# A hybrid decoder step: the bonus product placed behind the transposes, longer step distances, and a memory operand that takes over the input operand's halves

## Chip, cores and metric

The kernel runs on one core of one Trainium2 chip. The metric is the device time of one execution in microseconds (us); of several runs the median is given.

## The reference, cut to what matters here

One decoder layer for 256 prompt tokens and 8 sequences of 8 new tokens (320 tokens, 2048 wide). One projection with `w_in` gives the columns of a convolution group and of a time-mix group; their outputs are joined, projected, and followed by cross-attention into 256 memory tokens and a gated FFN. The change touches the time-mix group, whose 16 heads of 64 columns run a recurrence, and the memory keys:

```
def wkv_step(S, inp):
    r, w, k, v, a, b = inp
    sa = jnp.einsum('bhij,bhj->bhi', S, a)
    S = S * w[:, :, None, :] + sa[..., None] * b[:, :, None, :] + v[..., None] * k[:, :, None, :]
    y = jnp.einsum('bhij,bhj->bhi', S, r)
    return S, y
...
bonus = jnp.sum(rh * kh * heads(jnp.broadcast_to(p['r_k'].astype(f32), r.shape)), axis=-1, keepdims=True) * vh
out = (yn + bonus.reshape(b_, t_, W)) * g
...
def memory_kv(mem, p):
    m = rms_norm(mem, p['norm_mem'])
    k = (m @ p['w_k']).reshape(b_, N_MEM, XA_HEADS, XA_HEAD_DIM)
    v = (m @ p['w_v']).reshape(b_, N_MEM, XA_HEADS, XA_HEAD_DIM)
```

## The kernel before

**Weights.** Every large product is float32 carried as two float16 parts. A piece of a weight, 128 x 1024 float32, is loaded by SP into one of three buffers of the tag `raw`; ACT rounds it to `whi` (L154) and DVE computes the remainder `wlo` (L155). PE then runs three matmuls per 128 x 128 block: high by high, high by low, low by high (`dense_steps`, result `acc`). The input operand `h1`, transposed and split the same way, holds 16 blocks of 320 tokens in one tile.

**The recurrence** (L364 to L1073, about 95 to 705 us of the span) is one block in which the order of PE is the order in which the program issues instructions; the other engines and SP's queue are ordered by the framework's scheduler. Two things are interleaved there. The main line is dense work: `weights` (L1040) runs, four times, the r, k and v columns of two head pairs (`columns`) and two convolution blocks of 128 columns (`conv_dense`); then `memory` (L1046) runs the memory tokens' transposes (`memo_steps`, L903, PE result `pm`, split by ACT L918 and DVE L919 into `memo`) and the products with `w_k` (`mem_steps`, L928, result `acck`). The small work runs as streams: generators that issue a few instructions and then `yield d`, the step distance. A counter `clock[0]` advances with every matmul by its modelled length, and a stream is resumed between two dense steps once the counter has passed its last stop plus d. So a distance is PE work put between a product and the next product that needs what other engines make of it. When the real engines take longer than the distance, PE waits, since its order is fixed.

**The streams.** `prepare` (L482) makes the operands of one pair of heads, eight times: among them `kt` (POOL, L561), the bonus operand `k` (DVE, L562), `kh` (DVE, L570 and L571), then the bonus product

```
        yield 9.12
        pb_ = etile("pbon")
        mm(pb_[:, :T], bones, k2, True, True)
        bon = rb.tile([P, T], F32, tag="bon", bufs=3, name="bon")
        V.tensor_tensor(bon, pb_[:, :T], v, ALU.mult)
```

and then the transposes `px` of v and kt, of bt, and of v's and kh's sample columns. `etile` hands out one single PSUM bank (tag "x", one buffer), which every product of `prepare` uses in turn: the next one can start when the last has been read. `mtile` hands out five banks (tag "m"). `pair` (L595) runs the recurrence of a pair in chunks of 64 tokens: `invert` (L364; `psZ`, then DVE `zc`, then `psX`, then DVE `Tc` L400 and its transposition L401, four levels for the prompt), `prompt_part` (L661; four chunks of `pX`, ACT `x`, `pU`, DVE `u` L679, `pSc`), `sample_part` (L708) and the output (`pYt`). Two pairs are under way at a time, each of the two streams doing four pairs. The convolution's taps (DVE, L821, 31 for each of 8 blocks) are streams as well.

**The turn to the memory products.** When `conv_dense(7)` has been issued, a tile `memo` takes the place of `h1` in memory, so its first write has to wait until the last product has read `h1`. `memory` then issues four steps of transposes, each followed by `clock[0] += 1.0`, then the `w_k` products with the four other steps between them. The memory tiles `xm` use the same three `raw` buffers as the weights; the rest of the tile (`kvst`) holds results on the way out.

Of the kernel before, what the change touches and what calls it, by code (L numbers as in the profile page):

```python
# [9 lines left out]
F32 = mybir.dt.float32  # L10
# [36 lines left out]
def hybrid_step_kernel(ctx: ExitStack, tc: tile.TileContext, I, O):  # L47
# [137 lines left out]

    def opn(t):
        return lambda k: (t[:, k, 0, :], t[:, k, 1, :])

# [5 lines left out]
    def rows_in(pool, psum, loads, gcol, op, ssq, take):  # L194
        tl = []
        for j, (src, rows) in enumerate(loads):
            tl.append((pool.tile([P, D], F32, name=f"xt{j}"), rows))
        for q in range(4):
            qc = slice(q * 512, (q + 1) * 512)
            with tc.high_priority(offset=(2 * AHEAD if q == 0 else AHEAD)):  # L200
                for (xt, rows), (src, _) in zip(tl, loads):
                    SP.dma_start(xt[:rows, qc], src[:, qc])
            with tc.high_priority(offset=600):
                for f in range(4 * q, 4 * q + 4):
                    ps = psum.tile([P, 512], F32, tag="m", bufs=5, name="psn")
                    c = 0
                    for xt, rows in tl:
                        turn(ps[:, c:c + rows], xt[:rows, f * P:(f + 1) * P], ident[:rows, :rows])
                        c += rows
                    A.activation(op[:, f, 0, :c], ps[:, :c], AF.Copy, scale=gcol[:, f:f + 1])  # L210
                    V.scalar_tensor_tensor(op[:, f, 1, :c], ps[:, :c], gcol[:, f:f + 1], op[:, f, 0, :c], ALU.mult, ALU.subtract)
            take(q)
            for j, (xt, rows) in enumerate(tl):
                jk = pool.tile([P, 512], F16, tag="njk", bufs=2, name="njk")
                sq = A.activation(jk[:rows], xt[:rows, qc], AF.Square, accum_out=ssq[:rows, j, q:q + 1])
                if q in (0, 1, 2, 3):
                    late(sq)
# [4 lines left out]
    opA = tc.alloc_tile_pool(name="opA", bufs=1, side="right")  # L222
    h1 = opM.tile([P, KD, 2, T], F16, tag="h", name="h1")
    rwmix = opA.tile([P, 8, 2, T], F16, name="rwmix")
# [6 lines left out]
    with tc.tile_pool(name="p0", bufs=1, side="right", reuse_waits="tile") as p0:  # L231
# [12 lines left out]
        xp, xs_ = I["x_prompt"][0], I["x_sample"].rearrange("b t d -> (b t) d")  # L244
        rows_in(p0, psA, [(xp[0:128], 128), (xp[128:256], 128), (xs_, 64)], gx[:, 0:16], h1, xss, lambda q: [next(first_) for _ in range((8, 8, 8, 0)[q])])
        ldm = vr.tile([26, P], F32, name="ldm")
# [117 lines left out]
    def invert(A_, GG, nm, C, nlev):  # L364
# [17 lines left out]
        for lev in range(1, min(nlev, 5)):  # L382
# [10 lines left out]
            V.tensor_tensor(zm, psZ[:C, :nm * 16].rearrange("p (a c) -> p a c", c=16), CM[:C, lev].unsqueeze(1).broadcast_to([C, nm, 16]), ALU.mult)  # L393
            yield 3.16
            psX = mtile("psX")
# [5 lines left out]
            V.transpose(Gf, Tf)  # L401
            yield 3.78
        for q, r in enumerate(blk):
# [78 lines left out]
    def prepare(i, r, k, v):  # L482
# [79 lines left out]
        V.scalar_tensor_tensor(k2, r, vR["r_k"][:, c], k2, ALU.mult, ALU.mult)  # L562
        yield 9.12
        pb_ = etile("pbon")
        mm(pb_[:, :T], bones, k2, True, True)
        bon = rb.tile([P, T], F32, tag="bon", bufs=3, name="bon")
        V.tensor_tensor(bon, pb_[:, :T], v, ALU.mult)
        pcs = PS[:, :, 8:9].broadcast_to([P, NB, NT])
        kh = ra.tile([P, 2, NS], F32, tag="kh", name="kh")
        V.tensor_tensor(kh[:, 0].rearrange("p (b e) -> p b e", e=NT), sm(kt), pcs, ALU.mult)  # L570
        V.tensor_tensor(kh[:, 1].rearrange("p (b e) -> p b e", e=NT), sm(bt), pcs, ALU.mult)  # L571
        yield 0.71

# [5 lines left out]
        A.activation(tvkb[:, 0:2].rearrange("p z c f -> p (z c f)"), px, AF.Copy)  # L579
        yield 1.39  # L580
        px = etile("px")
        for ch in range(2):
            turn(px[:, ch * P:(ch + 1) * P], bt[:, ch * P:(ch + 1) * P], ident)
        A.activation(tvkb[:, 2].rearrange("p c f -> p (c f)"), px[:, 0:256], AF.Copy)
        yield 1.21

# [4 lines left out]
        A.activation(ts_[0:64, 0], px[0:64, 0:P], AF.Copy)  # L591
        A.activation(ts_[:, 1], px[:, P:2 * P], AF.Copy)
        return AR, bt, kt, bon, tvkb, ts_, pc

    def pair(i, AR, bt, kt, bon, tvkb, ts_, pc):  # L595
# [65 lines left out]
        def prompt_part():  # L661
            Sbd = Ssc = None
            for ch in range(4):
# [9 lines left out]
                A.activation(x[xr_], px[xr_, 0:P], AF.Copy)  # L673
                yield 1.5
                pu = mtile("pU")
# [5 lines left out]
                for hc in hcs:  # L681
                    mm(ps[hc, 0:64], tk[xr_, m, hc], tv[xr_, m, hc], True, False, True, 2)
                yield 1.1
                for hc in hcs:
# [13 lines left out]
                A.activation(Y[yr_, m, :], px[yr_, 0:P], AF.Copy)  # L698
                yield 1.5
            px = mtile("pSt")  # L700
# [200 lines left out]

    mst = cst.tile([P, 2, 8], F32, name="mst")
    def memo_steps():  # L903
        for q2 in range(2):
            for j in range(2):
                with tc.high_priority(offset=AHEAD):
# [4 lines left out]
                for q in range(2 * q2, 2 * q2 + 2):  # L911
                    px = mtile("pm")
                    for z in range(4):
                        turn(px[:, z * P:(z + 1) * P], xm[:, (4 * (q % 2) + z) * P:(4 * (q % 2) + z + 1) * P], ident)
                    cols = slice(j * P, (j + 1) * P)
                    for z in range(4):
                        f = 4 * q + z
                        A.activation(memo[:, f, 0, cols], px[:, z * P:(z + 1) * P], AF.Copy, scale=gx[:, 16 + f:17 + f])  # L918
                        V.scalar_tensor_tensor(memo[:, f, 1, cols], px[:, z * P:(z + 1) * P], gx[:, 16 + f:17 + f],  # L919
                                               memo[:, f, 0, cols], ALU.mult, ALU.subtract)  # L920
                    yield
# [6 lines left out]
    def mem_steps(src, dst, ns, psum):  # L928
        for n in ns:
            accs = [psum.tile([P, 512], F32, tag="acc", name="acck", **({"bufs": 2} if psum is psA else {})) for _ in range(2)]  # L930
            for k0 in range(0, KD, 2):
                hi, lo = wpiece(src, k0, 2, [(n * 512, 512)])
                for j in range(2):
                    for k in range(2):
                        kt, c, cols = k0 + k, slice(k * 512, (k + 1) * 512), slice(j * P, (j + 1) * P)
                        mm(accs[j], memo[:, kt, 0, cols], hi[:, c], kt == 0, False)
                        mm(accs[j], memo[:, kt, 1, cols], hi[:, c], False, False)
                        mm(accs[j], memo[:, kt, 0, cols], lo[:, c], False, kt == KD - 1)
                        yield 1.5
            for j in range(2):  # L940
                kv = kvst[:, j]
                A.activation(kv, accs[j], AF.Copy, scale=mst[:, j, 7:8])  # L942
# [97 lines left out]
    def weights():  # L1040
        for q in range(4):
            yield from columns(q)
            yield from conv_dense(2 * q)
            yield from conv_dense(2 * q + 1)

    def memory():  # L1046
        ms, ks = memo_steps(), mem_steps(I["w_k"][0], O[10], range(4), psA)
        for _ in range(4):
            next(ms)
            clock[0] += 1.0  # L1050
            yield
        for n in range(32):
# [12 lines left out]
    with tc.manual_schedule(engines={mybir.EngineType.PE}):  # L1065
        for a_ in (first_stage(), second_stage(0), second_stage(1)):
            spawn(a_)
        drive(weights())
        hm_ = opM.tile([P, KD * 2 * T], F16, tag="h", name="memo")
        memo = hm_[:, 0:KD * 2 * NPR].rearrange("p (k y t) -> p k y t", y=2, t=NPR)  # L1070
        kvst = hm_[:, KD * 2 * NPR:].bitcast(F32).rearrange("p (j c) -> p j c", c=512)
        drive(memory())
# [568 lines left out]
```

## Time and profile before

| | |
|---|---|
| median of the runs | 2090.84 us (2090.81 to 2093.16, 3 runs) |
| the profiled execution: time, span of its trace | 2092.7 us, 2090.9 us |
| mean granted clock | 0.989 |
| PE busy, share of the span | 2007.5 us (96%) |
| DVE busy | 1396.2 us (67%) |
| ACT, POOL busy | 992.6 us (47%), 591.9 us (28%) |

Everything below was read from the profiled execution. Busy shares are averages over stages that differ, so the views are taken by stretch: first what share of each stretch PE works, then what each of its waits is for, then the clock that PE was granted, and last the timelines of single places. "Idle before <-releaser" names the engine and result whose arrival ended a wait.

### The profile page before, as it was taken

What the parts mean: (1) busy time and instruction counts of PE and PEld (TensorE: products, weight loads), DVE (VectorE), ACT (ScalarE), POOL (GpSimd) and SP (SyncE); (2) the same over time, 40 slices, a digit from 0 to 9 for tenths busy, and PEclk for the clock granted to TensorE, in tenths of its full rate; (3) what the DMA queues carried; (4) which work ended last, traced back from release to release, by engine and by line L of the source; (5) the groups of instructions that cost most, each with busy time, mean ns of one, the idle gap of its engine ahead of it and who ended that gap; (6) DMA issues with size and microseconds to landing.
All of it is one profiled execution on the core that took longest, in us unless ns stands there. A gap on an engine that the chain in (4) does not pass through costs nothing.

```text
span 2090.9 us, 44949 instructions
## 1 busy us (share of the span) xinstructions
PE 2007.5 (96%) x17941; PEld 1393.0 (67%) x17941; DVE 1396.2 (67%) x2479; ACT 992.6 (47%) x1710; POOL 591.9 (28%) x908
## 2 busy tenths in 40 slices
PE   8989999898899999989999999999999999999998
PEld 6756666565454576566677667777777777777777
DVE  5698787986876635977774596666666666444344
ACT  5444445344545544756663454444444444533332
POOL 3635436344022111300001242444444444000000
PEclk9999999999999999999999999999999999999999
DMA  6543334332546765767775445555555555555554
GB/s 188 149 117 101 85 99 112 98 95 65 155 135 208 232 211 176 237 211 243 249 231 162 143 136 163 163 162 163 163 162 162 162 162 162 147 161 162 154 147 144
DMA packets 301998, 333.34 MB, mean 159 GB/s; under 512 B 33882, under 2 KB 227237, under 8 KB 301764
## 3 DMA queue, kind: packets, MB, share of 16 engines
q1 hardware_dynamic: 301788, 330.46, 52.6%
q8 instruction: 141, 2.31, 0.4%
q14 instruction: 69, 0.57, 0.1%
HBM read 319.90 MB, written 11.22 MB: 158 GB/s over the span
## 4 chain that ended last, share of the span: by engine, by line
PE 74%; DVE 11%; DMA 7%; ACT 3%; issue 3%; POOL 2%; SPq 0%; DVEq 0%; POOLq 0%; ACTq 0%
PE acc L57 59%; PE acck L57 5%; DVE wlo L155 3%; DMA rawkv<-in_cache_mem_v_dram 2%; PE pX L57 1%; DVE cvmix L821 1%; ACT whi L154 1%; DVE vl L1260 1%; DMA out_dram<-fo 1%; DMA raw<-in_w_v_dram 1%; PE pk L61 1%; DMA rawkv<-out_dram 1%; DMA raw<-in_w_k_dram 1%; DVE xr L1141 1%; PE psX L57 1%
## 5 line engine op out<-in xcount | busy, mean ns | idle before, releaser
L57 PE MATMUL acc<-h,whi 128*128 128x320 f16 (+1 forms) x4736 | 979.9, 301 | 11.7 <-DVE h L1143 3.7
L155 DVE SCALAR_TENSOR_TENSOR wlo<-raw,whi 128x1024 f16<-128x1024 f32 (+1 forms) x512 | 627.5, 1228 | 473.3 <-ACT whi L154 467.7
L57 PEld LDWEIGHTS <-whi 128*128 128x128 f16 (+1 forms) x7080 | 685.6, 99 | 277.5 <-issue 16.3
L154 ACT ACTIVATE whi<-raw 128x1024 f16<-128x1024 f32 (+1 forms) x512 | 533.0, 1043 | 599.6 <-PE acc L57 497.6
L57 PE MATMUL acc<-h,wlo 128*128 128x320 f16 (+1 forms) x2368 | 701.2, 300 | 0.2 <-DVE wlo L155 0.2
L57 PEld LDWEIGHTS <-wlo 128*128 128x128 f16 (+1 forms) x3540 | 348.4, 98 | 142.4 <-issue 7.1
L57 PE MATMUL acc<-act,whi 128*128 128x320 f16 x1320 | 270.3, 299 | 0.0
L57 PE MATMUL acc<-act,wlo 128*128 128x320 f16 x660 | 196.3, 299 | 0.0
L57 PE MATMUL acck<-whi,memo 128*128 128x512 f16 x512 | 152.6, 383 | 1.3 <-ACT memo L942 1.3
L821 DVE SCALAR_TENSOR_TENSOR cvmix<-GX,cdw,cvmix 128x320 f32<-128x320 f32 x240 | 140.7, 586 | 2.2
L1490 POOL COPY nF<-U 128x9 f32<-128x9 f32 x88 | 50.3, 571 | 302.3 <-DVE U L1489 299.4
L57 PEld LDWEIGHTS <-memo 128*128 128x128 f16 x768 | 72.9, 99 | 83.0 <-issue 4.4
L1487 POOL COPY U<-stF 128x16 f32<-128x16 f32 x88 | 125.9, 1436 | 0.8 <-ACT stF L1475 0.8
L1125 POOL TENSOR_TENSOR sums<-sums,bsq 128x320 f32<-128x320 f32 x33 | 37.9, 1149 | 241.3 <-ACT bsq L1119 239.6
L57 PE MATMUL acck<-wlo,memo 128*128 128x512 f16 x256 | 96.3, 382 | 0.3 <-DVE wlo L155 0.3
L1495 DVE SCALAR_TENSOR_TENSOR C<-U,fdw,C 128x336 f32<-128x336 f32 x176 | 91.8, 564 | 0.0
L1493 ACT ACTIVATE C<-U,fdw 128x336 f32<-128x336 f32 x88 | 56.0, 660 | 34.8 <-DVE U L1489 34.8
L1488 DVE TENSOR_TENSOR U<-acc,rs 128x256 f32<-128x256 f32 x88 | 36.9, 420 | 39.5 <-PE acc L57 39.5
L1260 DVE SCALAR_TENSOR_TENSOR vl<-rawkv,vh 128x1024 f16<-128x1024 f32 x31 | 37.2, 1223 | 30.0 <-ACT vh L1259 29.9
L1211 POOL CAST qs<-qf 128x64 f16<-128x64 f32 x16 | 10.0, 623 | 161.1 <-ACT qf L1208 161.1
L57 PE MATMUL acc<-oopb,whi 128*128 128x320 f16 x256 | 53.7, 299 | 1.0 <-DVE oopb L191 1.0
L57 PE MATMUL acc<-cvmix,whi 128*128 128x320 f16 x256 | 52.1, 299 | 1.5 <-ACT memo L942 1.5
(466 smaller groups left out, 2519.4 us busy)
## 6 DMA issues: line engine op xcount, KB each, us to landing
raw<-in_w_up_dram SPq DMA_DIRECT2D x352, 256.0 KB
raw<-in_w_down_dram SPq DMA_DIRECT2D x71, 512.0 KB
raw<-in_w_in_dram SPq DMA_DIRECT2D x52, 512.0 KB
raw<-in_w_in_dram SPq DMA_DIRECT2D x64, 256.0 KB
raw<-in_w_k_dram SPq DMA_DIRECT2D x32, 512.0 KB
raw<-in_w_v_dram SPq DMA_DIRECT2D x32, 512.0 KB
raw<-in_w_out_dram SPq DMA_DIRECT2D x32, 512.0 KB
rawkv<-in_cache_mem_k_dram SPq DMA_DIRECT2D x32, 512.0 KB
```

The costliest lines, as they stand in the source:

```text
L57: pe[0] = TE.matmul(out, lhsT=lhsT, rhs=rhs, start=start, stop=stop, skip_group_check=skip)
L61: pe[0] = TE.transpose(out, in_, idn)
L154: A.activation(hi[:, :n], raw[:, :n], AF.Copy, scale=SW)
L155: V.scalar_tensor_tensor(lo[:, :n], raw[:, :n], SW, hi[:, :n], ALU.mult, ALU.subtract)
L821: late(V.scalar_tensor_tensor(o_, i_, cdw[:, c, j:j + 1], o_, ALU.mult, ALU.add))
L1125: (V if f > 11 else G).tensor_tensor(ssum, ssum, sq, ALU.add)
L1260: V.scalar_tensor_tensor(vl, raw, SX, vh, ALU.mult, ALU.subtract)
L1487: G.tensor_copy(us[:, :, 0:2], stF[:, :, :, j])
L1488: V.tensor_tensor(U[:, 2:258], acc[:, 0:256], rf[:, 0:256], ALU.mult)
L1490: G.tensor_copy(nF[:, :, 0, j], U[:, 256:338:10])
L1493: A.activation(c, U[:, 0:336], AF.Identity, bias=fdw[:, 3, j:j + 1], scale=fdw[:, 0, j:j + 1])
L1495: V.scalar_tensor_tensor(c, U[:, t_:t_ + 336], fdw[:, t_, j:j + 1], c, ALU.mult, ALU.add)
```

## The change

Instruction counts stay the same on every engine. There are three parts.

1. In `prepare` the two `kh` products are issued ahead of the 9.12 distance; the bonus product goes behind all transposes and gets a bank of `mtile`.
2. Distances: in `invert` 3.16 becomes 3.5 and 3.78 becomes 4.2; in `prepare` the 0.71 behind the bonus goes, 1.39 becomes 1.6, 1.21 becomes 1.5, and 0.5 is added ahead of the bonus product and behind it; in `prompt_part` 1.5 becomes 1.8 (twice a chunk) and 1.1 becomes 1.5.
3. `h1` becomes two tiles of eight blocks each, `h0` and `h1`. `memo` becomes two halves that take their places one by one, and the first four steps of `memo_steps` are issued within the second half of `conv_dense(7)`, one after every four dense steps; `clock[0] += 1.0` goes.

```diff
     def opn(t):
+        if isinstance(t, list):
+            return lambda k: (t[k // 8][:, k % 8, 0, :], t[k // 8][:, k % 8, 1, :])
         return lambda k: (t[:, k, 0, :], t[:, k, 1, :])
...
-    h1 = opM.tile([P, KD, 2, T], F16, tag="h", name="h1")
+    h1 = [opM.tile([P, KD // 2, 2, T], F16, tag=f"h{q}", name="h1") for q in range(2)]
...
             V.tensor_tensor(zm, psZ[:C, :nm * 16].rearrange("p (a c) -> p a c", c=16), CM[:C, lev].unsqueeze(1).broadcast_to([C, nm, 16]), ALU.mult)
-            yield 3.16
+            yield 3.5
...
             V.transpose(Gf, Tf)
-            yield 3.78
+            yield 4.2
...
         V.scalar_tensor_tensor(k2, r, vR["r_k"][:, c], k2, ALU.mult, ALU.mult)
-        yield 9.12
-        pb_ = etile("pbon")
-        mm(pb_[:, :T], bones, k2, True, True)
-        bon = rb.tile([P, T], F32, tag="bon", bufs=3, name="bon")
-        V.tensor_tensor(bon, pb_[:, :T], v, ALU.mult)
         pcs = PS[:, :, 8:9].broadcast_to([P, NB, NT])
         kh = ra.tile([P, 2, NS], F32, tag="kh", name="kh")
         V.tensor_tensor(kh[:, 0].rearrange("p (b e) -> p b e", e=NT), sm(kt), pcs, ALU.mult)
         V.tensor_tensor(kh[:, 1].rearrange("p (b e) -> p b e", e=NT), sm(bt), pcs, ALU.mult)
-        yield 0.71
+        yield 9.12
...
         A.activation(tvkb[:, 0:2].rearrange("p z c f -> p (z c f)"), px, AF.Copy)
-        yield 1.39
+        yield 1.6
...
         A.activation(tvkb[:, 2].rearrange("p c f -> p (c f)"), px[:, 0:256], AF.Copy)
-        yield 1.21
+        yield 1.5
...
         A.activation(ts_[:, 1], px[:, P:2 * P], AF.Copy)
+        yield 0.5
+        pb_ = mtile("pbon")
+        mm(pb_[:, :T], bones, k2, True, True)
+        bon = rb.tile([P, T], F32, tag="bon", bufs=3, name="bon")
+        V.tensor_tensor(bon, pb_[:, :T], v, ALU.mult)
+        yield 0.5
         return AR, bt, kt, bon, tvkb, ts_, pc
...
                 A.activation(x[xr_], px[xr_, 0:P], AF.Copy)
-                yield 1.5
+                yield 1.8
...
-                yield 1.1
+                yield 1.5
...
                 A.activation(Y[yr_, m, :], px[yr_, 0:P], AF.Copy)
-                yield 1.5
+                yield 1.8
...
+    memo, kvst = [None, None], [None, None]
+
+    def memo_half(q):
+        hm_ = opM.tile([P, KD * T], F16, tag=f"h{q}", name="memo")
+        memo[q] = hm_[:, 0:KD * NPR].rearrange("p (k y t) -> p k y t", y=2, t=NPR)
+        kvst[q] = hm_[:, KD * NPR:].bitcast(F32)
+
     def memo_steps():
         for q2 in range(2):
+            memo_half(q2)
...
             yield from conv_dense(2 * q)
-            yield from conv_dense(2 * q + 1)
+            if q < 3:
+                yield from conv_dense(2 * q + 1)
+
+        last_ = conv_dense(7)
+        for _ in range(2 * KD // 2):
+            next(last_)
+            yield
+        for _ in range(4):
+            for _ in range(4):
+                next(last_, None)
+                yield
+            next(ms)
+        yield from last_
+
+    ms = memo_steps()
 
     def memory():
-        ms, ks = memo_steps(), mem_steps(I["w_k"][0], O[10], range(4), psA)
-        for _ in range(4):
-            next(ms)
-            clock[0] += 1.0
-            yield
+        ks = mem_steps(I["w_k"][0], O[10], range(4), psA)
```

**Order on PE, the seventh pair's bonus.** Before, `pbon` stands first, the `px` transposes behind it (names: `pSt`, `pY` are products of the pair ahead; `vx` is v):

```order
L57 MATMUL pbon<-k_7047,bones 128x320
L61 MATMUL pSt<-ident,Ssc 64x128
L57 MATMUL pY<-XT,sel 64x128
L57 MATMUL pY<-u,AMs_524 64x64
L57 MATMUL pY<-ts,AMs_524 64x64
L57 MATMUL pY<-u,AMs_524 64x64
L57 MATMUL pY<-ts,AMs_524 64x64
L61 MATMUL px<-ident,vx 128x128 x2
L61 MATMUL px<-ident,kt 128x128 x2
```

After, on the same pair, the last `px` transposes come first and `pbon` behind the next pair's `pX`:

```order
L61 MATMUL px<-ident,vx 64x128
L61 MATMUL px<-ident,kh 128x128
L57 MATMUL pX<-XT,sel 64x128
L57 MATMUL pX<-ts,AMs_525 64x64 x2
L57 MATMUL pX<-tvkb,AM_523 64x64 x4
L57 MATMUL pX<-S_7152,AR 128x128
L57 MATMUL pbon<-k_6960,bones 128x320
```

The first pair of transposes now stands some fifty rows ahead of `pbon`; the other seven pairs moved in the same way.

**Order on PE at the turn to the memory products.** Before, behind the last `acc` of `conv_dense(7)` stand the memory transposes `pm` in four groups between small products, and then the first key product:

```order
L61 MATMUL pco<-ident,GN 30x128
L61 MATMUL pco<-ident,ctl 64x128
L61 MATMUL pm<-ident,xm 128x128 x4
L57 MATMUL pA<-AR,bt 64x128 x2
L57 MATMUL pA<-AR,kt 64x128 x2
L57 MATMUL psX<-zc,Gc 32x16 x16
L61 MATMUL pm<-ident,xm 128x128 x8
L57 LDWEIGHTS memo
L57 MATMUL acck<-whi,memo 128x512
```

After, three groups of `pm` stand within `conv_dense(7)`, and the last rows ahead of the key product are

```order
L57 MATMUL pA<-AR,bt 64x128 x4
L57 MATMUL pA<-AR,kt 64x128 x4
L57 LDWEIGHTS whi
L57 MATMUL acc<-h_173,whi 128x320
L57 LDWEIGHTS whi
L57 MATMUL acc<-h_173,whi 128x320
L57 LDWEIGHTS wlo
L57 MATMUL acc<-h_173,wlo 128x320
L61 MATMUL pm<-ident,xm 128x128 x8
L57 LDWEIGHTS memo
L57 MATMUL acck<-whi,memo 128x512
```

Dense products stand up to the last eight transposes, and the first key product follows these at once. From the second group of `pm`, the last reader of the first memory piece, to the key product stand eight blocks of three dense products, `pbon`, `psX`, four `pA` and twelve more `pm`.

**Order of SP's queue at the same place.** Before (`xm` is a piece of the memory tokens, `co` the convolution's state on its way out):

```order
L908 DMA xm<-in_mem_prompt_dram 128x1024 x2
L150 DMA raw<-in_w_k_dram 128x2x512
L805 DMA out_dram<-co 30x128
L807 DMA out_dram<-co 8x128 x7
L150 DMA raw<-in_w_k_dram 128x2x512
L908 DMA xm<-in_mem_prompt_dram 128x1024
L807 DMA out_dram<-co 8x128
L150 DMA raw<-in_w_k_dram 128x2x512 x6
```

After:

```order
L920 DMA xm<-in_mem_prompt_dram 128x1024 x2
L150 DMA raw<-in_w_k_dram 128x2x512 x2
L920 DMA xm<-in_mem_prompt_dram 128x1024
L150 DMA raw<-in_w_k_dram 128x2x512
L809 DMA out_dram<-co 30x128
L811 DMA out_dram<-co 8x128 x8
L150 DMA raw<-in_w_k_dram 128x2x512 x8
```

The first `xm` stands between the last four pieces of `w_in` (seven rows further ahead), and two pieces of `w_k` are issued ahead of the `co` transfers and of the fourth `xm`. PE's order is the same in both kernels up to about 95 us of the span and again from about 705 us on.

## Rows read from the trace of the kernel before

**Rows 1.** Windows; columns: stretch, length, busy PE, PEld, DVE, ACT, POOL, clock, DMA, GB/s.

```profile
95.00:500.00 405.00, 380.73 (x5245) 259.73 (x5244) 336.71 (x747) 177.83 (x418) 182.88 (x276) 0.98 0.37 99
500.00:565.00 65.00, 51.28 (x772) 31.14 (x770) 55.30 (x139) 34.07 (x81) 11.74 (x20) 0.92 0.39 118
...
521.00:530.50 9.50, 6.74 (x131) 5.14 (x129) 8.18 (x26) 6.64 (x18) 1.10 (x2) 0.92 0.22 62
```

**Rows 2.** Waits of PE from 95 to 500 us: waited-for result, total, times, longest.

```profile
PE px L61 <- DVE bon L567: 7.0, 4, 2.6
PE psZ L57 <- DVE Tc L400: 3.6, 3, 1.9
PE pSc L57 <- DVE u L679: 2.6, 4, 1.0
PE pbon L57 <- DVE k L562: 2.3, 2, 1.2
```

**Rows 3.** Waits of PE from 500 to 565 us.

```profile
PE px L61 <- DVE bon L567: 2.6, 1, 2.6
...
PE psZ L57 <- DVE Tc L400: 2.5, 1, 2.5
```

**Rows 4.** Windows again, where the granted clock is below full.

```profile
125.00:130.00 5.00, 5.00 (x55) 3.14 (x55) 5.00 (x11) 2.59 (x8) 3.91 (x8) 0.66 0.02 4
387.50:392.50 5.00, 3.20 (x42) 2.12 (x42) 4.42 (x10) 0.96 (x2) 0.00 (x0) 0.66 0.56 136
472.50:482.50 10.00, 9.07 (x58) 5.50 (x59) 3.59 (x8) 3.17 (x9) 3.95 (x6) 0.66 0.33 97
...
557.50:565.00 7.50, 6.15 (x70) 3.11 (x70) 6.05 (x13) 1.65 (x3) 0.86 (x1) 0.77 0.34 101
```

**Rows 5.** PE's timeline from 385 us: start, length, line, work, [idle before <-releaser].

```profile
385.15 0.78 PE L57 MATMUL pbon<-k,bones 128*128 128x320 f32 x2 [1.05 <-DVE k L562]
...
389.30 0.69 PE L61 MATMUL px<-ident,vx 128*128 128x128 f32 x2 [2.56 <-DVE bon L567]
...
391.95 0.62 PE L57 MATMUL psX<-zc,Gc 32*32 32x16 f32 x32
```

**Rows 6.** DVE's timeline in the same stretch.

```profile
384.93 0.54 DVE L821 SCALAR_TENSOR_TENSOR cvmix<-GX,cdw,cvmix 128x320 f32<-128x320 f32 x1
...
386.52 1.14 DVE L821 SCALAR_TENSOR_TENSOR cvmix<-GX,cdw,cvmix 128x320 f32<-128x320 f32 x1
387.59 0.21 DVE L393 TENSOR_TENSOR zc<-psZ,CM 128x64 f32<-128x64 f32 x1
...
388.76 0.48 DVE L567 TENSOR_TENSOR bon<-pbon,vx 128x320 f32<-128x320 f32 x1
```

**Rows 7.** POOL's timeline in the same stretch.

```profile
381.10 1.10 POOL L561 TENSOR_TENSOR kt<-k,IP 128x320 f32<-128x320 f32 x1
...
385.51 1.81 POOL L842 TENSOR_TENSOR cth<-cth,rh 128x320 f32<-128x320 f32 x1 [2.24 <-ACT cth L839]
```

**Rows 8.** PE's timeline at the last pair's end.

```profile
632.27 0.58 PE L61 MATMUL pYt<-ident,Y 128*128 128x128 f32 x3
```

**Rows 9.** PE's timeline at the end of the memory products.

```profile
706.20 0.38 PE L57 MATMUL acck<-wlo,memo 128*128 128x512 f16 x1
...
706.85 0.38 PE L57 MATMUL acck<-wlo,memo 128*128 128x512 f16 x1
```

**Rows 10.** PE's timeline where the memory keys begin.

```profile
520.45 0.30 PE L57 MATMUL acc<-h,wlo 128*128 128x320 f16 x1
...
520.86 0.30 PE L57 MATMUL acc<-h,wlo 128*128 128x320 f16 x1
...
530.46 1.06 PE L57 MATMUL acck<-whi,memo 128*128 128x512 f16 x2
```

**Rows 11.** The transfers that SP issued there.

```profile
529.84 0.41 SPq L150 DMA_DIRECT2D raw<-in_w_k_dram  x1
```

**Rows 12.** DVE's timeline at the split of that piece.

```profile
534.80 1.23 DVE L155 SCALAR_TENSOR_TENSOR wlo<-raw,whi 128x1024 f16<-128x1024 f32 x1 [0.45 <-ACT whi L154]
```

More of the change, by code (lines that the diff above doesn't have):

```diff
@@ L209, in rows_in @@
                         c += rows
-                    A.activation(op[:, f, 0, :c], ps[:, :c], AF.Copy, scale=gcol[:, f:f + 1])
-                    V.scalar_tensor_tensor(op[:, f, 1, :c], ps[:, :c], gcol[:, f:f + 1], op[:, f, 0, :c], ALU.mult, ALU.subtract)
+                    oh, ol = op(f)
+                    A.activation(oh[:, :c], ps[:, :c], AF.Copy, scale=gcol[:, f:f + 1])
+                    V.scalar_tensor_tensor(ol[:, :c], ps[:, :c], gcol[:, f:f + 1], oh[:, :c], ALU.mult, ALU.subtract)
             take(q)
@@ L244, in hybrid_step_kernel @@
         xp, xs_ = I["x_prompt"][0], I["x_sample"].rearrange("b t d -> (b t) d")
-        rows_in(p0, psA, [(xp[0:128], 128), (xp[128:256], 128), (xs_, 64)], gx[:, 0:16], h1, xss, lambda q: [next(first_) for _ in range((8, 8, 8, 0)[q])])
+        rows_in(p0, psA, [(xp[0:128], 128), (xp[128:256], 128), (xs_, 64)], gx[:, 0:16], opn(h1), xss, lambda q: [next(first_) for _ in range((8, 8, 8, 0)[q])])
         ldm = vr.tile([26, P], F32, name="ldm")
@@ L916, in memo_steps @@
                     for z in range(4):
[L917 to L920, printed above, removed]
+                        f, mo = 4 * q + z, memo[q2][:, 4 * (q % 2) + z]
+                        A.activation(mo[:, 0, cols], px[:, z * P:(z + 1) * P], AF.Copy, scale=gx[:, 16 + f:17 + f])
+                        V.scalar_tensor_tensor(mo[:, 1, cols], px[:, z * P:(z + 1) * P], gx[:, 16 + f:17 + f],
+                                               mo[:, 0, cols], ALU.mult, ALU.subtract)
                     yield
@@ L935, in mem_steps @@
                         kt, c, cols = k0 + k, slice(k * 512, (k + 1) * 512), slice(j * P, (j + 1) * P)
-                        mm(accs[j], memo[:, kt, 0, cols], hi[:, c], kt == 0, False)
-                        mm(accs[j], memo[:, kt, 1, cols], hi[:, c], False, False)
-                        mm(accs[j], memo[:, kt, 0, cols], lo[:, c], False, kt == KD - 1)
+                        mo = memo[kt // 8][:, kt % 8]
+                        mm(accs[j], mo[:, 0, cols], hi[:, c], kt == 0, False)
+                        mm(accs[j], mo[:, 1, cols], hi[:, c], False, False)
+                        mm(accs[j], mo[:, 0, cols], lo[:, c], False, kt == KD - 1)
                         yield 1.5
             for j in range(2):
-                kv = kvst[:, j]
+                kv = kvst[j]
                 A.activation(kv, accs[j], AF.Copy, scale=mst[:, j, 7:8])
@@ L1068, in hybrid_step_kernel @@
         drive(weights())
-        hm_ = opM.tile([P, KD * 2 * T], F16, tag="h", name="memo")
-        memo = hm_[:, 0:KD * 2 * NPR].rearrange("p (k y t) -> p k y t", y=2, t=NPR)
-        kvst = hm_[:, KD * 2 * NPR:].bitcast(F32).rearrange("p (j c) -> p j c", c=512)
         drive(memory())
```

## The prediction

> **What bounds the kernel now.** I read the windows by stage first, then PE's waits, then the granted clock, then the timelines of two places. PE's order differs only between about 95 and 705 us of the span, so all that the change can do lies there. In the two stretches of it where PE has gaps, PE works 380.73 of 405 us and 51.28 of 65 us [rows 1]: 24.3 and 13.7 us are idle. The rest is PE's own work, which the change leaves as it is, matmul for matmul. So time can come only from the idle 38.0 us and from stretches in which PE works at a lower clock, and time can be lost by new gaps. DVE, with 336.71 of 405 and 55.30 of 65 us busy [rows 1], is what most gaps end on: four transposes waited 7.0 us for the bonus and two bonus products 2.3 us for their operand, four times `pSc` waited for `u` (2.6 us), three times `psZ` for `Tc` (3.6 us) [rows 2]; from 500 us on another 2.6 us for the bonus and 2.5 us for `Tc` [rows 3]. The clock shows a second cost. The mean granted clock is 0.66 in the first three windows of [rows 4] and 0.77 in the last, so part of each ran at the 1.2 GHz level and not at 2.4 GHz: 0.34 of 5 us, or 1.7 us, is lost in the windows at 125 and 387.5, twice that at 472.5, and 0.23 of 7.5, again 1.7, at 557.5. Two more windows of five microseconds, at 515 and 527.5, read like the one at 387.5. That makes seven losses of 1.7 us, 11.9 us, as the 0.98 and 0.92 of the two stretches say [rows 1]. The windows at 387.5, 515 and 527.5 lie at waits that the change addresses (the bonus, twice, and the memory split); those at 125, 472.5 and 557.5 follow waits for `mid`, for the state and for a later split of `memo`, which it leaves.
>
> **Part 1, the bonus.** The sixth pair shows it [rows 5 to 7]. The bonus product waited 1.05 us for its operand, was done at 385.93, and the transposes behind it waited 2.56 us until 389.30 [rows 5], because both use the one bank "x" and DVE read the bonus only from 388.76 to 389.24 [rows 6]. DVE was not late with that one instruction: it stood in a queue with taps and the inversion's `zc` that had no gap. The transposes themselves need v and `kt`, and POOL finished `kt` at 382.20 [rows 7], 1.9 us before PE reached the bonus (385.15 less 1.05). With the transposes first, all they need is there, ACT empties the bank, and PE no longer meets DVE. The removed waits are 7.0 + 2.6 + 2.3 = 11.9 us [rows 2, 3]. I take three quarters, 9 us: DVE has no less to do, and something else of it will be late in a quarter of the cases. The bounds are 11.9 (all) and 0 (PE runs forward only to the next operation of that queue). The `kh` products are issued earlier, but DVE already did them ahead of the bonus, so they cost nothing; their cover is DVE's order itself, and without it two operations of 0.2 us would stand ahead of `bon`. The bonus now holds one of five banks "m" from its product to DVE's read, 4.1 us in the case shown (385.15 to 389.24). If the other four are in use, the wait comes back: at most the 7.0 + 2.6 = 9.6 us of all five, at least 0. I take one of the five, 1.9 us, as cost.
>
> **Part 2, the distances.** Longer distances remove a wait only by their own length: 0.42 us for each of the four waits on `Tc`, 0.4 us for each of the four on `u`, together 3.3 us; I take 3. The full waits, 3.6 + 2.5 + 2.6 = 8.7 us, are the upper bound, 0 the lower. The cost is a longer chain. A pair gets four inversion levels of 0.76 and four chunks of 1.0 us longer, 7.04 us of the program's clock, and a stream does four pairs, so 28.2 us; `prepare` gets 0.79 longer, eight times. That is hidden: the last pair's output begins at 632.27 [rows 8], while the memory products run until 706.85 [rows 9], 74 us later. Without that slack the 28 us would stand at the end of the stage.
>
> **Part 3, the memory operand.** The last product that reads the input operand starts at 520.86, 0.41 us behind the like one ahead of it, and the first key product starts at 530.46 [rows 10]. Between 521.0 and 530.5 PE works 6.74 us [rows 1], mostly transposes and small products that are done somewhere in any case; 2.8 us are idle, while DVE works 8.18 us, much of it the split of `memo`. With the first four steps inside the last convolution block, eight blocks of three dense products (0.41 us each) and the small products, some 8 us, stand between the transposes that free the first key piece's buffer and the first key product. A piece takes 6.2 us from its transfer's issue at 529.84 [rows 11] to the end of its split at 536.03 [rows 12], so the first one is in time by some 2 us, and in the order after, `w_k` pieces stand ahead of the `co` transfers in SP's queue, which can only help them. I take 2 of the 2.8 us, since DVE's work at this place stays; the upper bound is 2.8. The lower is -18: the five pieces around the turn (two of `w_in`, three of `w_k`) share three buffers with the memory tiles, and each could be exposed by 6.2 less its use on PE, four blocks of 0.65 us [rows 9], that is 3.6 us. The new shape of the operand's tile changes no instruction and costs nothing.
>
> **Part 4, the clock.** Three of the seven losses of 1.7 us lie at waits that go: 5.1 us. Bounds: 0 and all seven, 11.9.
>
> **Sum.** 9 + 3 + 2 + 5.1 - 1.9 = 17.2 us less. The profiled execution took 2092.7 us, 1.9 above the median of 2090.84 and inside the runs' spread, so the gain is set against the median: **2073.6 us**. All upper bounds with no cost give 35.3 (2055.5), all lower ones a loss of 27.6 (2118.4).
>
> **Rivals.** *All removed waits stay away.* Then the waits give 11.9 + 3.3 + 2.8 and the clock, with few gaps left, all of 11.9: 29.9, or 2060.9 us. For it: `zc` was ready at 387.80 [rows 6], four microseconds before `psX` used it [rows 5], so nothing late stood right behind the bonus. Against: what comes ahead of the windows at 125, 472.5 and 557.5 us is not touched, and they hold four of the seven clock losses.
>
> *DVE is the bound.* Every wait in [rows 2, 3] ends on DVE, which in the case shown worked without a gap. Then PE only reaches the next DVE result earlier and waits there. The bonus gives 2, the distances 0, the memory 2, the clock one unit, less 1.9: 3.8 us, or 2087.0. For it: a tap next to POOL's product took 1.14 us, where the one before took 0.54 [rows 6], as POOL worked from 385.51 to 387.32 [rows 7]; such delays stay. Against it: 68 of 405 us of DVE are idle, the work in the way was taps that may come later, and `zc` was early. The Trainium skill ("SBUF — State Buffer", section "SBUF: two separate sides") says that DVE and GpSimd lock a shared port pair for a whole instruction when DVE reads two operands from SBUF, so the tap would start at 387.32 and end at 387.86; it ended at 387.66, so the trace agrees within 0.2 us. By that rule each of eight pairs would keep 0.6 us of a DVE delay, 4.8 us in all, and the sum would be 12.4 (2078.4) where the rows alone give 17.2.
>
> *Slower: the buffers starve.* If the memory tiles hold two of the three weight buffers through the turn, one buffer serves weights in series. Five pieces each expose 3.6 us and each gap costs a clock unit of 1.7: 26.5 us. With 9 and 3 from parts 1 and 2, 3.4 of clock and -1.9, the time is 13.0 longer, 2103.8. It decides once it costs over 13.5 + 4.2 = 17.7 us, 3.5 a piece. For it: the first memory tile now stands between the last pieces of `w_in`. Against: the margin of 2 us worked out above, and small products between the key products stretch a piece's use.
>
> **How the numbers follow.** A measurement of this kernel can tell 0.2%, 4.2 us, from no change. The forecast has 0.56 (its own range 2066 to 2082), all waits gone 0.12, DVE the bound 0.22, slower 0.10. DVE's 2087.0 lies on the border of 2086.7, so 0.12 of it counts as faster and 0.10 as the same. Faster: 0.56 + 0.12 + 0.12 = 0.80; same 0.10; slower 0.10. The range 2059 to 2089 takes in the first three cases and some two microseconds beyond them; it leaves out the slower case and the ends of the bounds, together under 0.2.
>
> **What would show it.** It is right with these rows: no wait of `px` for `bon`; the idle time between 95 and 565 us down from 38.0 to about 25; the first key product within a microsecond of the last transposes; full clock around 390, 517 and 530 us. Part 1 is wrong if the waits for `Tc`, `u` or `zc` grow by what those for `bon` lose, or if products of tag "m" wait for `bon`. Part 3 is wrong if `acc` or `acck` waits for a split near the turn. If PE's idle time falls but the clock windows stay, part 4 is wrong, and the time is near 2079.

## The result and the profile after

The changed kernel takes 2080.07 us (median of 4 runs, 2078.16 to 2081.68) against 2090.82 of before: a ratio of 0.9946, 95% interval 0.9929 to 0.9963, or 10.7 us less (7.7 to 14.8). Timed again beside other kernels it gave 0.9957 (0.9944 to 0.9971). The prediction was 17.2 us less, 2073.6, in a range of 2059 to 2089. Its profiled execution is the fastest of the four, 2078.16 us, 14.5 less than the profiled one of before, so about 4 of these 14.5 us are which executions were profiled.

The two traces are compared from 95 us to the first product `acc<-cvmix`, behind which the order of PE is the same again (PE is TensorE, DVE is VectorE, ACT ScalarE and POOL GpSimd). That product starts at 708.73 us before and at 692.71 after. Executions are not at quite the same point of the program at 95 us: the `pn` products that stand there come 0.3 us earlier after the change, and in the versions below up to 0.7 us earlier or 1.6 us later than before, so a stage time is good to about that. First the windows of before, cut at the 1152nd `acc<-h` product, at the last one of the convolution, at the first key product, at the 192nd, and at `acc<-cvmix` (columns as in [rows 1]):

```profile
95.00:267.00 172.00, 158.32 (x2282) 108.11 (x2281) 147.84 (x328) 74.36 (x172) 76.79 (x116) 0.99 0.36 98
267.00:521.00 254.00, 237.98 (x3150) 162.04 (x3148) 206.55 (x457) 112.21 (x263) 114.75 (x173) 0.97 0.35 96
521.00:530.46 9.46, 6.70 (x131) 5.10 (x129) 8.13 (x26) 6.64 (x18) 1.10 (x2) 0.92 0.22 62
530.46:609.30 78.84, 73.31 (x932) 39.39 (x931) 62.96 (x146) 39.81 (x88) 10.11 (x12) 0.97 0.51 148
609.30:708.73 99.43, 95.66 (x513) 45.43 (x512) 64.97 (x89) 54.64 (x79) 19.39 (x16) 1.00 0.66 203
```

The same windows of the changed kernel, cut at the same products:

```profile
95.00:257.63 162.63, 153.54 (x2078) 105.59 (x2077) 142.86 (x313) 73.17 (x169) 75.35 (x115) 0.98 0.38 103
257.63:517.36 259.73, 244.08 (x3398) 168.40 (x3396) 213.62 (x484) 117.80 (x280) 117.47 (x174) 0.97 0.35 96
517.36:518.22 0.86, 0.86 (x10) 0.85 (x8) 0.86 (x4) 0.61 (x3) 0.00 (x0) 1.00 0.96 341
518.22:591.98 73.76, 70.03 (x988) 37.81 (x986) 62.76 (x150) 39.88 (x88) 10.51 (x12) 1.00 0.53 154
591.98:692.71 100.73, 96.04 (x533) 46.40 (x532) 66.85 (x95) 55.77 (x84) 21.47 (x18) 1.00 0.67 200
```

Length less PE's busy time is what PE stood idle: before 13.7, 16.0, 2.8, 5.5 and 3.8 us, together 41.8; after 9.1, 15.7, 0, 3.7 and 4.7, together 33.2. So 8.6 of the 16.0 us are idle time. PE's busy time falls by 7.4 us (571.97 to 564.55) with the same instructions. In the second stretch, where the most was expected, 16.0 became 15.7. The waits of PE from 95 to 500 us after the change (columns as in [rows 2]) say why:

```profile
PE psZ L57 <- DVE Tc L383: 3.9, 2, 1.9
PE pSc L57 <- DVE Zs L695: 3.4, 2, 3.2
PE pSc L57 <- DVE u L683: 2.7, 1, 2.7
PE psX L57 <- DVE zc L396: 2.1, 3, 1.0
```

All waits of `px` and `pbon` on DVE [rows 2] are gone, 9.3 us. In their place stand others on DVE: `Tc` of the inversion's start (L383), `Zs`, `zc`, which were 1.0, 0 and 0.4 us before. A single wait for the bonus is left, of `pA`, 0.4 us.

The granted clock of the changed kernel, in windows of its low stretches (six stretches before the cut; two shown):

```profile
210.00:215.00 5.00, 5.00 (x33) 3.35 (x33) 1.80 (x6) 2.25 (x6) 0.97 (x1) 0.66 0.67 165
...
390.00:397.50 7.50, 6.59 (x126) 4.33 (x128) 7.37 (x21) 2.91 (x6) 0.42 (x1) 0.77 0.24 72
```

Each costs 1.7 us as in [rows 4]. Before there were seven such losses up to `acc<-cvmix`, three of them from 515 us on; after there are six, all of them ahead of 475 us. Of the busy time's 7.4 us one loss explains 1.7; the rest is spread over many small groups.

### The profile page after: what moved, and what is told of

It is laid out like the page before. It is cut to its first block, busy times and chain, and to the rows that moved or that the text cites. A ratio compares the mean times of both kernels' runs of the same rounds, so it can differ in the third digit from the quotient of the medians.

```text
span 2076.4 us, 44951 instructions
## 1 busy us (share of the span) xinstructions
PE 1998.6 (96%) x17941; PEld 1391.3 (67%) x17941; DVE 1394.8 (67%) x2479; ACT 991.5 (48%) x1710; POOL 591.4 (28%) x908
## 4 chain that ended last, share of the span: by engine, by line
PE 77%; DVE 11%; DMA 5%; ACT 2%; issue 2%; POOL 2%; SPq 0%; DVEq 0%; POOLq 0%; ACTq 0%
PE acc L57 60%; PE acck L57 6%; DVE wlo L155 2%; DMA rawkv<-in_cache_mem_v_dram 2%; DVE cvmix L825 1%; PE pX L57 1%; PE pk L61 1%; DVE vl L1280 1%; ACT whi L154 1%; PE psZ L57 1%; DVE xr L1161 1%; PE pSn L57 1%; PE psX L57 1%; ACT vh L1279 1%; PE pos L57 1%
## 5 line engine op out<-in xcount | busy, mean ns | idle before, releaser
L1508 DVE TENSOR_TENSOR U<-acc,rs 128x256 f32<-128x256 f32 x88 | 36.7, 418 | 39.4 <-PE acc L57 39.4
L335 POOL TENSOR_TENSOR pb<-pb,rh 128x256 f32<-128x256 f32 (+1 forms) x28 | 27.6, 986 | 98.4 <-ACT pb L332 85.0
```

What stands on the lines that cost most here:

```text
L335: G.tensor_tensor(pb[:w, 1:257], pb[:w, 1:257], rh[:w, 0:256], ALU.mult)
L1508: V.tensor_tensor(U[:, 2:258], acc[:, 0:256], rf[:, 0:256], ALU.mult)
```

## The experiments

Ratios are to the kernel before on the same chip. "Stage" is from 95 us to the first `acc<-cvmix`, with PE's idle time in it, both from the windows of the one profiled execution. The versions were timed in three groups, each beside the kernel before, whose median was 2092.71, 2090.84 and 2091.58 us. The expectations name 40 us for the idle time of before and 31.7 for that after the change; by the windows it is 41.8 and 33.2.

| version | ratio (95% interval) | stage, us | idle, us | PE busy, us |
|---|---|---|---|---|
| before | 1 | 613.7 | 41.8 | 572.0 |
| part 1 (bonus) alone | 0.9967 (0.9954 to 0.9979) | 605.9 | 36.7 | 569.2 |
| part 2 (distances) alone | 1.0016 (1.0006 to 1.0026) | 616.9 | 41.5 | 575.4 |
| part 3 (memory) alone | 0.9965 (0.9953 to 0.9978) | 602.9 | 34.6 | 568.4 |
| only the bonus's bank | 0.9958 (0.9946 to 0.9970) | 598.9 | 32.4 | 566.6 |
| parts 1 and 3 | 0.9960 (0.9948 to 0.9972) | 603.5 | 32.4 | 571.0 |
| parts 1 and 2 | 0.9977 (0.9962 to 0.9992) | 612.2 | 34.7 | 577.5 |
| parts 2 and 3 | 1.0015 (1.0006 to 1.0024) | 615.6 | 40.6 | 574.9 |
| bank and part 3 | 0.9952 (0.9939 to 0.9966) | 597.5 | 32.9 | 564.6 |
| bank, part 3, inversion's distances | 0.9993 (0.9978 to 1.0008) | 607.0 | 38.7 | 568.4 |
| the change | 0.9946 (0.9929 to 0.9963) | 597.7 | 33.2 | 564.6 |
| the change again | 0.9957 (0.9944 to 0.9971) | 599.6 | 33.0 | 566.6 |

**The parts alone.** Three kernels with one part each, and a fourth that only moves the bonus to another bank.

Part 1 alone is the hunk on `prepare`, without its longer distances:

```diff
-        yield 9.12
-        pb_ = etile("pbon")
...
-        yield 0.71
+        yield 9.12
...
+        yield 0.5
+        pb_ = mtile("pbon")
...
+        yield 0.5
         return AR, bt, kt, bon, tvkb, ts_, pc
```

> Only part 1 of the change: the bonus product behind the transposes, in a bank of tag m (its two distances of 0.5 with it, the other distances as before). Parts add up: no wait of px for bon (9.6 us before) and none of pbon for k (2.3 us), idle time of PE between 95 us and the first cvmix product down from 40 to about 32 us, 2084 to 2087 us. DVE is the bound: the waits come back as waits for Tc, u, zc or S, idle time stays at 38 us or above, 2089 to 2092 us.

It gave 2086.83 us against 2092.71. Two of the longest waits of its trace from 95 to 565 us:

```profile
PE pSc L57 <- DVE u L680: 3.3, 4, 1.4
PE pX L57 <- DVE S L695: 3.1, 2, 2.8
```

No wait for the bonus is left. Of the 11.9 us in [rows 2, 3], 5.1 show up as less idle time; waits for `u` and `S` grew (2.6 and 1.8 us before). The time is that of the first theory, the idle time lies between the two.

Part 2 alone:

```diff
-            yield 3.16
+            yield 3.5
...
-            yield 3.78
+            yield 4.2
...
-        yield 1.39
+        yield 1.6
...
-        yield 1.21
+        yield 1.5
...
-                yield 1.5
+                yield 1.8
...
-                yield 1.1
+                yield 1.5
...
-                yield 1.5
+                yield 1.8
```

> Only part 2: the longer distances in the inversion, in prepare's transposes and in the prompt's chunks; the bonus stays where it was. Parts add up: waits for Tc and u shrink by about 3 us, those for bon stay at 8 us or more, 2087 to 2089 us. DVE is the bound: what is gained there is lost at other DVE results, 2090 to 2092 us, with px still waiting for bon.

It is slower, 2096.23 us, by an interval that excludes no change; neither theory named that. The waits of its trace from 95 to 565 us:

```profile
PE px L61 <- DVE bon L567: 5.7, 4, 1.8
PE pXR L57 <- ACT S0T L638: 3.7, 1, 3.7
PE pU L57 <- DVE u L679: 3.4, 1, 3.4
...
PE psZ L57 <- DVE Tc L380: 2.3, 3, 1.2
PE pYt L61 <- DVE Y L760: 2.3, 1, 2.3
PE psZ L57 <- DVE Tc L400: 1.9, 2, 1.0
...
PE pSc L57 <- DVE u L679: 0.6, 2, 0.4
```

The waits that the distances aim at did shrink: `psZ` for `Tc` of L400 from 3.6 + 2.5 us [rows 2, 3] to 1.9, `pSc` for `u` from 2.6 to 0.6. But `pXR`, `pU` and `pYt` now wait 9.4 us for `S0T`, `u` and `Y`, waits that are not in the trace of before, and `psZ` waits 2.3 us, for 1.0, for the first `Tc` of an inversion (L380). The idle time stays (41.5 for 41.8) and the busy time grows by 3.4 us, and the windows show why:

```profile
138.00:147.00 9.00, 7.74 (x63) 4.77 (x64) 6.88 (x15) 3.25 (x4) 1.56 (x1) 0.62 0.41 121
209.50:222.00 12.50, 10.21 (x97) 6.84 (x98) 7.65 (x17) 3.88 (x9) 5.49 (x5) 0.59 0.17 46
```

The second of these, 12.5 us at a clock of 0.59 (0.41 of 12.5, 5.1 us lost), begins in the wait of 3.4 us for `u`. It is not this one execution alone: over the eleven that were timed the mean granted clock is 0.9865, over the eighteen of the kernel before beside them 0.9898. The difference is 0.0033 of 2096 us, an estimate of 6.9 us, more than the 3.5 that were lost. So what the distances cost alone is clock, with as much idle time as before.

Part 3 alone is the hunks on `opn`, `h1`, `memo_half`, `memo_steps`, `weights` and `memory`:

```diff
-    h1 = opM.tile([P, KD, 2, T], F16, tag="h", name="h1")
+    h1 = [opM.tile([P, KD // 2, 2, T], F16, tag=f"h{q}", name="h1") for q in range(2)]
...
+            memo_half(q2)
...
+            next(ms)
+        yield from last_
```

> Only part 3: the operand in halves and the first four memory steps inside the last convolution block. Parts add up: the first key product starts within 2 us of the last product of the convolution (9.5 us before), one clock loss of 1.7 us fewer, 2086 to 2089 us. Turn gives nothing: the small products that filled the 9.5 us stand elsewhere, the splits of memo block DVE as before, 2090 to 2092 us.

2084.96 us against 2092.71, 7.3 us by the ratio where the first theory named 2 to 5. Its timeline at the turn (columns as in [rows 5]), and its wait for the bonus from 95 to 565 us:

```profile
519.74 0.30 PE L57 MATMUL acc<-h,wlo 128*128 128x320 f16 x1
...
521.50 0.59 PE L57 MATMUL acck<-whi,memo 128*128 128x512 f16 x2
```

```profile
PE px L61 <- DVE bon L570: 5.8, 4, 1.8
```

The key products begin 1.8 us behind the convolution, where it was 9.6 [rows 10]. The waits for the split of `memo` are gone too. Before, from 95 to 565 us, there were 5.1 us of them, mostly in these two (the others 0.7 and 0.2):

```profile
PE psZ L57 <- DVE memo L919: 2.6, 1, 2.6
PE psX L57 <- DVE memo L919: 1.6, 1, 1.6
```

Only the bank, all else as before:

```diff
-        pb_ = etile("pbon")
+        pb_ = mtile("pbon")
```

> The bonus product stays ahead of the transposes, but gets a bank of tag m. If the shared bank was the cause of the 9.6 us, px no longer waits for bon and the time is that of part 1 alone, less at most the 2.3 us of pbon waiting for k: 2085 to 2089 us. If the place ahead of the transposes was the cause, px still waits and the time is 2090 to 2092 us.

2085.65 us. The window of its stage, then PE's timeline at the sixth pair, then DVE's:

```profile
95.00:693.90 598.90, 566.55 (x7000) 357.57 (x6997) 488.35 (x1040) 288.06 (x620) 222.75 (x319) 0.99 0.44 123
```

```profile
381.37 1.40 PE L57 MATMUL pbon<-k,bones 128*128 128x320 f32 x2 [1.05 <-ACT whi L154]
384.16 0.43 PE L61 MATMUL px<-ident,vx 128*128 128x128 f32 x2
```

```profile
382.74 1.14 DVE L821 SCALAR_TENSOR_TENSOR cvmix<-GX,cdw,cvmix 128x320 f32<-128x320 f32 x1
...
384.98 0.48 DVE L567 TENSOR_TENSOR bon<-pbon,vx 128x320 f32<-128x320 f32 x1
```

DVE does the same work in the same order as in [rows 6], and reads the bonus 3.6 us after the product began, as before. But the transposes start at 384.16, ahead of that, without a wait. No `px` waits for `bon` any more, and the stage's idle time is 9.4 us less, about the 9.6 us of these waits [rows 2, 3]. The shared bank was what tied PE to DVE's queue; the place ahead of the transposes, in a bank of its own, does not. One line gives what the whole first part gives, within the intervals. Whether the new place alone, in the shared bank, would also do it was not run. The profiled execution is the fastest of its five; of its 5.4 us less busy time, three clock losses fewer (four for seven) are 5.1.

**Pairs of parts.** Each is the change less one part; the fourth kernel joins the one-line edit of the bank with part 3.

> The change without its longer distances (parts 1 and 3). If parts add up, -0.33% and -0.35% give about 0.9932 of before, faster than the whole change (0.9946), and the distances cost it some 3 us as they do alone (1.0016). If the distances belong to part 1 (they need the bonus out of the way to pay), this is slower than the whole change: 0.996 or above.

0.9960 is not the sum of the parts, 0.9932. It lies where the second theory put it, but the whole change (0.9946 and 0.9957) is not faster by more than the intervals allow. Inside the whole change the distances neither cost nor give anything that these runs can tell. The three parts alone would multiply to 0.9948, and the whole change gives that; but this pair, and parts 2 and 3 below, are each some 0.3% off their products, so the match is no sign that the parts add up.

> The change without part 3 (bonus and distances). If parts add up: 0.9967 times 1.0016, about 0.998, the key products again starting some 10 us behind the last convolution product. If the distances pay once the bonus is out of the way: below 0.9967.

0.9977 fits the sum of the parts, 0.998; that the distances pay is not borne out. The profiled execution is the longest of its twelve runs (2093.08 us; they begin at 2081.01), so its stage is not typical. PE's busy time of 577.5 us in it is the clock, here the stretch around the turn, where 0.09 of 100 us, 9 us, was lost:

```profile
500.00:600.00 100.00, 91.05 (x1182) 51.11 (x1180) 80.17 (x192) 50.63 (x114) 16.73 (x22) 0.91 0.45 128
```

> The change without part 1 (distances and memory operand), the bonus where it was. If parts add up: about 0.998, px waiting for bon again. If the gain of the memory part came only from how it shifted the bonus waits (9.6 to 5.8 us in that run): 0.9995 or above.

1.0015: the memory part, worth 0.35% alone, is worth nothing next to the distances as long as the bonus waits. The longest waits are those of part 2 alone:

```profile
PE px L61 <- DVE bon L570: 5.9, 4, 1.9
PE pXR L57 <- ACT S0T L641: 3.7, 1, 3.7
```

> Only the bank of the bonus product, in its old place, and part 3; no distances, no reordering. If the bank is what paid and parts add up: -0.42% and -0.35%, about 0.9923, faster than the whole change. If the reordering is needed next to the memory part: no faster than the change without its distances.

0.9952, where 0.9923 was the sum. So the gains do not add: once the bonus is out of the way, the memory part adds 0.06% to the bank's 0.42%, within the intervals. The waits say why. Of those for `memo` 3.5 us become 0.5, but `pbon` waits longer for its operand, here with the bank alone and then with both:

```profile
PE pbon L57 <- DVE k L562: 1.4, 2, 1.2
```

```profile
PE pbon L57 <- DVE k L565: 4.8, 3, 2.3
```

The idle time stays (32.4 and 32.9 us). This version has neither reordering nor distances, and is as fast as the whole change within what the runs can tell.

**Is DVE the bound?** Both kernels with 16 of the 31 taps of each block; the others are left out, so the convolution's values and what follows from them are not the reference's.

```diff
-        for j in range(CW):
+        for j in range(16):
             i_ = GX[:, :, j:j + NT]
```

> The kernel before with 16 of the 31 taps of each convolution block, 120 DVE instructions of 0.54 us fewer in the recurrence (the rest of the convolution is left out, so its output differs). If the bonus waits are DVE's queue: px waits for bon under 4 us instead of 9.6, idle time from 95 us to the first cvmix product under 25 instead of 40 us, 2070 us or less. If the single bank is slow by itself (product, read, release in turn, whatever DVE's load): px still waits 7 us or more, 2083 us or more.

> The changed kernel with 16 of the 31 taps of each convolution block (the rest is left out, its output differs). If what stays idle after the change (31.7 us) is DVE's queue: under 18 us, 2065 us or less. If it is the fixed length of the chains against the distances: 27 us or more, 2075 us or more.

The first gave 1.0009 (0.9999 to 1.0020), the second 0.9919 (0.9902 to 0.9935). Windows of the first and the second:

```profile
95.00:706.43 611.43, 572.85 (x7003) 360.81 (x7002) 433.37 (x923) 287.77 (x620) 209.80 (x320) 0.98 0.43 120
```

```profile
95.00:685.18 590.18, 561.50 (x6999) 357.22 (x6998) 429.44 (x922) 286.88 (x620) 212.49 (x319) 0.99 0.44 125
```

DVE works 57 us less in the stage in either, and PE's idle time falls from 41.8 to 38.6 and from 33.2 to 28.7 us. In the kernel before, `px` still waits for the bonus:

```profile
PE px L61 <- DVE bon L567: 7.2, 4, 2.6
```

DVE's timeline there shows that the run did not take away what stood in the way:

```profile
384.50 1.15 DVE L821 SCALAR_TENSOR_TENSOR cvmix<-GX,cdw,cvmix 128x320 f32<-128x320 f32 x1
385.57 0.21 DVE L393 TENSOR_TENSOR zc<-psZ,CM 128x64 f32<-128x64 f32 x1
385.70 1.12 DVE L821 SCALAR_TENSOR_TENSOR cvmix<-GX,cdw,cvmix 128x320 f32<-128x320 f32 x2
386.75 0.48 DVE L567 TENSOR_TENSOR bon<-pbon,vx 128x320 f32<-128x320 f32 x1
```

These are among the sixteen taps that stay. So neither theory stood as written: by its numbers (7.2 us of waits, 2094.22 us) the first run is the second theory's, but the bonus still came late by DVE's queue, so a bank that is slow by itself isn't shown. Of the second run the idle time (28.7 us) is the second theory's and the time, 2074.32 us, just below it. What the runs do show: DVE's total work is not the bound, since 57 us less of it in the stage left the time of the kernel before as it was and took 5 to 8 us off the changed one. The waits come from what stands ahead in DVE's queue at a place.

**A better version?** Bank and memory part, with the two longer distances of the inversion, and the change once more beside it.

```diff
-            yield 3.16
+            yield 3.5
...
-            yield 3.78
+            yield 4.2
```

> The bonus in its own bank at its old place, the memory part, and of the distances only those of the inversion (3.5 and 4.2). Waits for Tc were 5.3 us in the version without these distances. If they pay: about 0.993 and waits for Tc under 4 us. If the distances cost here as they did alone: 0.996 or above.

0.9993: the two numbers cost 8.6 us against the same kernel without them (0.9952, each beside its own kernel before; the intervals lie apart). Waits of its trace from 95 to 565 us:

```profile
PE psZ L57 <- DVE Tc L383: 4.2, 3, 2.1
PE psZ L57 <- DVE Tc L403: 3.6, 2, 2.8
PE pX L57 <- DVE S L697: 3.1, 2, 2.0
```

The waits for `Tc` did not shrink at all (1.0 and 5.3 us without the distances, 4.2 and 3.6 with them); they moved to another line of the inversion.

> The changed kernel as it is, beside the others of this call. 0.9935 to 0.9957 of before; within 0.1% of the version with the inversion's distances if the place of the bonus doesn't matter once it has its own bank.

0.9957, as named; the version with the inversion's distances was not within 0.1% of it, so the second half of the expectation failed. No version that was run beats the change clearly, and the bank with the memory part equals it with far less edited.

## Why the prediction was right, and where it was not

The sign and the range were right; the size was 17.2 us against 10.7. Of the four gains in the sum the bonus held, and the memory operand about; the distances and the clock, 8.1 us together, gave nothing that the runs can tell. That the time still lies in the range owes to the bonus and to the range's width. Of the signs named, no `px` waits for `bon`, and the first key product begins 0.9 us after the last transposes begin; but the idle time between 95 and 565 us is 27.8 us (22.8 to 500 us, 5.0 behind it) and not about 25, and the clock around 390 us is not full. Step by step:

- **The bonus**, 9 us less a cost of 1.9, and two of the clock's losses. The waits went as forecast, and the part alone gives 0.33%, 6.9 us. The cause was put in two places, order and bank; the runs show that the bank alone does it (8.8 us). The sign against this part, that the waits for `Tc`, `u` and `zc` grow by what those for the bonus lose, was met in part: up to 500 us those three grow by 2.7 us, and `Zs` by 3.4, where 9.3 went. In the changed kernel the bonus is read 4.5 us after its product began (PE's timeline, then DVE's):

```profile
384.22 0.81 PE L57 MATMUL pbon<-k,bones 128*128 128x320 f32 x2
...
389.26 0.33 PE L57 MATMUL pA<-AR,bt 64*64 64x128 f32 x3 [0.43 <-DVE bon L595]
```

```profile
388.73 0.48 DVE L595 TENSOR_TENSOR bon<-pbon,vx 128x320 f32<-128x320 f32 x1
```

  The cost of holding a bank of tag "m" was 0.43 us, a single wait, and not 1.9.

- **The distances**, 3 us. This step failed: "Longer distances remove a wait only by their own length", with only the chain's end as a cost. The named waits did shrink, but other results then meet PE late: 9.4 us in new waits in part 2 alone, with the clock lower, and 8.6 us slower in the bank version, with 5.8 us more idle time. A step that comes later by the program's clock is put among other dense products; that this is how the new waits come about is argued, not shown. What was late next was not asked for this part.

- **The memory operand**, 2 us. Alone it gave 7.3 us, and its idle time falls by 7.2. The term counted the turn's 2.8 us [rows 1] and left the later waits for `memo` as they were; alone, the part takes all 5.1 us of them away. `px` also waited less for the bonus, 5.8 us for 9.6, but `pbon` more for its operand, 4.8 for 2.6. With the bonus out of the way it adds little that can be measured, and in the whole change half of the wait for `memo` stays, 2.5 us, later in the order, as the changed kernel's timeline shows:

```profile
517.35 1.04 PE L61 MATMUL pm<-ident,xm 128*128 128x128 f32 x8
...
518.22 0.59 PE L57 MATMUL acck<-whi,memo 128*128 128x512 f16 x2
...
522.14 0.44 PE L57 MATMUL psZ<-Tc,AM 32*32 32x16 f32 x32 [2.53 <-DVE memo L931]
```

- **The clock**, 5.1 us. In the profiled execution 1.7. Of the three losses at waits that went, those at 515 and 527.5 are gone and the one at 387.5 is there again at 390, though `px` no longer waits there; others came, as the one at 210. In the second profile of the same kernel (the last row of the table) the clock is full around 390, and a loss stands at the turn, seven in all as before:

```profile
523.50:528.50 5.00, 5.00 (x80) 2.59 (x79) 4.12 (x18) 4.46 (x13) 0.79 (x2) 0.66 0.36 113
```

  The mean granted clock over all executions is 0.990, of the nine of the changed kernel as of the 64 of the kernel before that the versions were timed beside; 5.1 us would be 0.002 more. So nothing of this term shows. The step's error was to let a loss vanish with its wait and to count none for the waits that come.

Of the rivals, the fast one (2060.9) is out. DVE as the bound was priced at 3.8 us gained, and the measured 10.7 lies midway between that and the forecast; its mechanism, removed waits that come back at other DVE results, is what the waits of the changed kernel show in part, but DVE's total load as its ground is not borne out by the runs with sixteen taps. The starving buffers did not show: neither `acc` nor `acck` waits for a split at the turn. The rule of the Trainium skill ("SBUF — State Buffer", section "SBUF: two separate sides") on the port pair that DVE and GpSimd share gave 12.4 us, nearer to the result than the rows' 17.2. The stretched tap that it explains stands with the bank alone and with sixteen taps as well (1.14 us at 382.74, 1.15 at 384.50, where the like took 0.54), so the traces agree with the delay there. It doesn't come with every overlap: in the trace of before ten taps lie wholly within a GpSimd instruction, six of them within ones of six columns, and took 0.52 to 0.55 us. That the rule accounts for the difference was not tried.

## What to carry to other kernels

When an engine with a fixed order waits for a slower one, look first for a buffer that ties two unrelated things: giving the product a bank of another group was one line and did as much as moving it. Step distances in a fixed order are no local fix; here each set of them brought new waits elsewhere, so sum new waits along with the removed ones, look at the clock, and try them one at a time. Gains from waits that end on the same queue need not add: 0.33 and 0.35% alone made 0.40% together, 0.42 and 0.35% made 0.48%, and 0.35 and -0.16% made a loss of 0.15%. All three parts together gave about their sum, 0.4 to 0.5%, so one total that fits proves nothing.

## What was unexpected of the hardware

The same kernel's executions spread by up to 16 us (2082.87 to 2099.00 in the version with the inversion's distances, whose profiled one took 2084.38), more than the effect under study. In the profiled execution of parts 1 and 2, the longest of its kernel, PE's busy time in the stage was 577.5 us against 565 to 567 in the change and the two versions with the bank alone or with part 3, with the same instructions and the granted clock at 0.91 over a hundred microseconds in which PE was busy for 91. The clock makes a part of the spread. In the version with the inversion's distances the three shortest executions have a mean granted clock of 0.991 to 0.993, the seven above 2090 us one of 0.987 to 0.989; 0.005 of 2090 us between the shortest and the longest is, as an estimate, 10 of the 16 us. In the changed kernel (0.989 to 0.991) the two don't go together. What makes the rest was not tried.
